# A mixer's chain, attention and merges given steps one whole unit apart, with the order left to the scheduler

## The chip, the cores and the metric

The kernel runs on one core of one Trainium2 chip. The metric is the device time of one execution in microseconds (us), less is better. Three executions of the kernel before took 1160.99, 1154.00 and 1153.95 us, median 1154.0.

## The reference

One layer of a streaming encoder on a stream of 16 meta tokens and 512 frames, width 1024, fp32: a half-step SwiGLU feed-forward (FFN1, inner width 2816), a mixing of two head groups side by side, a second half-step SwiGLU (FFN2) and a final norm.

```python
h += 1/2 * SwiGLU(RMSNorm(h))
n = RMSNorm(h); z = n @ W_in
h += concat(rwkv_out, attn_out) @ W_out
h += 1/2 * SwiGLU(RMSNorm(h))
```

`rwkv_out` is the RWKV-7 recurrence, 8 heads of 64, one state of 64x64 per head:

```python
sa = jnp.einsum('bhvk,bhk->bhv', S, -kk_t)
S = (S * w_t[:, :, None, :]
     + sa[..., None] * (kk_t * a_t)[:, :, None, :]
     + v_t[..., None] * k_t[:, :, None, :])
y_t = jnp.einsum('bhvk,bhk->bhv', S, r_t)
```

followed by a norm per head, a bonus term and a gate. `attn_out` is attention with 8 query and 2 key heads, in chunks of 64 frames with a window of two chunks back, the meta tokens, ALiBi and one sink per head.

## The kernel before, in words

The stream is cut in two halves of tokens: half 0 (A: the meta tokens and frames 0 to 255, 272 columns) and half 1 (B: 256 columns). Everything is held transposed, features on the partitions. Each weight matrix lies in tiles ("units"), most of 128 output features by 1024 inputs. A unit's weights come by DMA (`raw`), are rounded by ACT to a high part (`whi`, L122), and DVE takes the rest as a low part (`wlo`, L125); both are read on the fast fp32r path. A unit is 24 matmuls of 256 or 272 columns for a half ("main matmuls"): 16 with `whi` against the high and the low part of the activations (L213, L214), 8 with `wlo` against the high part (L195, for the down projection L222). Three buffers each for `raw`, `whi`, `wlo` are made by `prep` three units ahead.

`drive` walks the list of units: FFN1 of A; then, between units of FFN1 of B, the units of `w_in` of A, the mixing of A and `w_out` of A; then `w_in` of B, the units of FFN2 of A beside the mixing of B, `w_out` of B, the rest. After each unit it calls `advance(cost)`, which lets the side generators go on. A generator has a credit: each unit adds its cost, a step takes what the step yields, and steps run while the credit is positive. There are two generators in a mixing:

- `rwkv` is first the inverse of 40 + 40 unit-triangular blocks of 32x32 (`tinv`, a DVE loop of 31 steps, L726 and L728), then a round trip of the result through DRAM, whose DMAs the ACT queue issues (L734 to L746), then two steps of 32x32 matmuls, L753 and L761, that merge the blocks to 64x64 (called the merge here). `chain` then walks five chunks (the 16 meta tokens or one more of 64, then 64 tokens each): `values` (64x64 matmuls L791 and L796 and four copies L799, L800 per chunk); L813 and L816, copied by L819 and added by L820; L828, copied by L830; then L838 to L848, the state update L851 and L852 and the output Y (L855, L856). A group norm follows each chunk: square L869, matmul L872, root L874, reciprocal L875, products L877 to L879, and its result is written by L881 (ACT, high part) and L882 (DVE, low part) into `n0a` or `n1a`, an input of `w_out`.
- `attention` walks four chunks of a half, each in two steps (`mp2`): scores L910, masks and maxima on DVE (L916 to L920), exponential on ACT (L924), reciprocal L928, scaling by ACT (L929), transposes L930 and L932, copies L937 and L939, products L942 and L945, then L950 and L951 into `n0b` or `n1b`, the other inputs of `w_out`.

`w_out` reads `WO = (4, 5, 6, 7, 0, 1, 2, 3)`: blocks 4 to 7 (attention) first, then 0 to 3 (chain).

PSUM has a pool of main accumulators (`big`), one-bank tiles `mx` (two buffers) and one two-bank tile `as` (one buffer, `banks()`), which attention uses for scores, transposes and products. `values` takes two `mx`.

The order of each engine's queue is not the program's: the tile scheduler places instructions by their dependences and by priorities, which `PRIO` raises by 100 for chain and norm.

Of the kernel before, what the change touches and what calls it, by code (L numbers as in the profile page):

```python
# [9 lines left out]
AF = mybir.ActivationFunctionType  # L10
# [24 lines left out]
WARM = 12  # L35
TIW, CHW, ATW = 1.4, 0.55, 0.9
NK = D // 128
# [31 lines left out]
class Prog:  # L69
# [96 lines left out]
    def advance(self, cost):  # L166
        for sd in list(self.sides):
            if sd not in self.sides:
                continue
            sd[1] += cost  # L170
            while sd[1] > 0:
                self.mark(self.ph or sd[2] if sd[2] == 'rwkv' else sd[2])
                with self.tc.high_priority(PRIO.get(self.ph if sd[2] == "rwkv" else "", PRIO[sd[2]])):
                    c = next(sd[0], None)
                if c is None:
                    self.sides.remove(sd)
                    break
                sd[1] -= c
# [525 lines left out]
    def tinv(self, hf, mp, tip):  # L704

        nc, A, V, P, PE, t, GT = self.nc, self.A, self.V, self.P, self.PE, self.t, self.GT
# [17 lines left out]
        for k in range(1, 32):  # L724
            m = tmp[:n2, :k * k].rearrange("g (j s) -> g j s", s=k)
# [21 lines left out]
        self.ph = 'tizo'  # L747
        yield 6.0
        pc = [(p, c, slice((p * 4 + c - 1) * 32, (p * 4 + c) * 32)) for p in range(4) for c in range(1, 5)]
# [5 lines left out]
        for h in range(2):  # L755
            (A.copy, V.tensor_copy)[h](out=Z[hr[h]], in_=bz[hr[h]])
        yield 2.0
        bo = self.mbank()
# [3 lines left out]
        for h in range(2):  # L762
            (A.copy, V.tensor_copy)[h](out=GT[hr[h], 4 * h:4 * h + 4, 1:5, 32:64],
                                       in_=bo[hr[h]].rearrange("p (h s t) -> p h s t", h=4, s=4))
        yield 2.0

    def chain(self, hf, st, mo, cp):

        A, V, P, PE, t, GT, S = self.A, self.V, self.P, self.PE, self.t, self.GT, self.S
# [3 lines left out]
        def step():  # L773

            for n_ in list(norms):
                if next(n_, None) is None:
                    norms.remove(n_)
# [4 lines left out]
        def values(n):  # L782


            slot, tok, C = chunks[n]
            UV, BT = t(cp, [128, 2, 4, 64], "UV", bufs=2), t(cp, [128, 2, 4, 64], "BT", bufs=2)
            vr = (slice(64, 64 + C), slice(0, C))
            bs = [self.mbank() for h in range(2)]
            for p in range(4):
# [13 lines left out]
        values(0)  # L803
        yield CHW
        hp = [(p, h) for p in range(4) for h in range(2)]
        for n, (slot, tok, C) in enumerate(chunks):
# [5 lines left out]
            for p, h in hp:  # L812
                PE.matmul(X[ur[h], cols(p)], gt(vr, h, p, 0), UV[vr[h], h, p], start=True, stop=True)  # L813
            if slot:
                for p, h in hp:
                    PE.matmul(Z[hs[h], cols(p)], self.AR[p][hs[h], slot, 0:64], S[hs[h], p], start=True, stop=True)  # L816
# [7 lines left out]
            step()  # L824
            yield 2 * CHW
            X = self.mbank()
            for p, h in hp:
                PE.matmul(X[ur[h], cols(p)], gt(ur, h, p, 0), Rs[ur[h], cols(p)], start=True, stop=True)  # L828
            for h in range(2):
                (A.copy, V.tensor_copy)[h](out=UV[ur[h], h], in_=X[ur[h], 0:256].rearrange("p (j c) -> p j c", j=4))  # L830
            step()
            yield CHW
            if n + 1 < len(chunks):
                values(n + 1)
            yield CHW
            X, Z = self.mbank(), self.mbank()
# [16 lines left out]
            if slot:  # L853
# [3 lines left out]
                norms.append(self.group_norm(st, mo, cp, Y, slice(64 * slot - 64, 64 * slot)))  # L857
            step()
            yield 2 * CHW
        self.ph = 'gn'  # L860
        while norms:
            step()
            yield 2.0

# [20 lines left out]
    def attention(self, hf, st, mo, ap_):  # L885
        A, V, P, PE, t = self.A, self.V, self.P, self.PE, self.t
        for ci in range(4):
            c = 4 * hf + ci
            nw = min(c + 1, 3)
            W = 17 + 64 * nw  # L890
# [13 lines left out]
            A.copy(out=VK[0:81, 0], in_=b[0:81, 0:128])  # L904
            yield ATW
            kss = (slice(0, 64), slice(64, 128))
            for mp2 in range(2):
                bs, rows = self.banks(), []
# [3 lines left out]
                for kv in range(2):  # L912
                    g, x = 2 * kv + mp2, bs[kv][:, 0:W]
                    s = t(ap_, [128, 209], "s", bufs=2)
                    m = t(ap_, [128, 4], "m", bufs=4)
# [5 lines left out]
                    rows.append((s, m))  # L921
                yield ATW
                for s, m in rows:
                    A.activation(s[:, 0:W], s[:, 0:W], AF.Exp, bias=m[:, 2:3], accum_out=m[:, 3:4])  # L924
                yield ATW
                b, bo = self.banks()
                for kv, (s, m) in enumerate(rows):
                    V.reciprocal(m[:, 3:4], m[:, 3:4])  # L928
                    A.activation(s[:, 0:W], s[:, 0:W], AF.Copy, scale=m[:, 3:4])  # L929
                    PE.transpose(b[0:81, 256 * kv:256 * kv + 128], s[:, 0:81], self.ident)  # L930
                    if nw > 1:
                        PE.transpose(b[0:W - 81, 256 * kv + 128:256 * kv + 256], s[:, 81:W], self.ident)  # L932
                yield ATW
                pTs = []
# [8 lines left out]
                if nw > 1:  # L943
                    for kv, ks in enumerate(kss):
                        PE.matmul(bo[ks, 0:128], VK[0:W - 81, 1, ks], pTs[kv][0:W - 81, 1], start=False, stop=True)  # L945
                yield ATW
                ms, ts = slice(2 * mp2, 2 * mp2 + 2), slice(64 * ci, 64 * ci + 64)
# [3 lines left out]
                V.tensor_tensor(out=ml, in0=ov, in1=mh.bitcast(F32), op=ALU.subtract)  # L951
                yield ATW

# [250 lines left out]
```

## Time and profile before

| | |
|---|---|
| Executions | 1160.99, 1154.00, 1153.95 us; median 1154.0 |
| Profiled execution | 1158.89 us, of which span on the core 1156.7 us |
| Mean granted clock of TensorE | 0.971 |
| Busy: PE, DVE, ACT, POOL | 1114.7, 826.4, 673.0, 36.4 us |
| ACT table loads for L395, L924, L874 | 25, 13, 5, at 1283 ns |

The span is the time from the first to the last instruction of the profiled execution; 2.2 us lie around it. PE is TensorE's matmul stream, which is pipelined: a busy window may hold matmuls 0.12 us apart or, at half of the granted clock, some 0.21 us apart. So for PE three things are read: idle time and its releaser, the granted clock of a window (PEclk, 1.00 is 2.4 GHz and 0.50 is 1.2 GHz), and the number of matmuls in it.

### The profile page before, as it was taken

How to read it: one execution, taken by the hardware profiler on the slowest of the kernel's cores; microseconds unless marked ns; L12 is line 12 of the kernel's file. 1: busy time of each engine (PE TensorE's matmuls, PEld its weight loads, DVE VectorE, ACT ScalarE, POOL GpSimd, SP SyncE). 2: the span in 40 equal slices, each digit the busy share in tenths (PEclk: the TensorE clock that was granted, in tenths of full speed). 3: DMA queues.
4: the chain of work that ended last, by engine and by line, in shares of the span. 5: the costliest groups of instructions: out<-in, count | busy, mean ns of one | idle time of the engine just before them, and what ended most of it. 6: DMA issues, size and time to landing. Idle time of an engine off the chain costs nothing.

```text
span 1156.7 us, 23838 instructions
## 1 busy us (share of the span) xinstructions
PE 1114.7 (96%) x9621; PEld 1043.9 (90%) x9621; DVE 826.4 (71%) x1533; ACT 673.0 (58%) x1162; POOL 36.4 (3%) x91
## 2 busy tenths in 40 slices
PE   8999999999999998999899999997999899999996
PEld 7999999998999997899899898997889898888885
DVE  7866566776778993356888777995356677777666
ACT  7544444686757645565567685574456366545453
POOL 0000000021000000000002000000000000000000
PEclk8999999999999998899899999998899899999999
DMA  7565655544446554223355445556224356676661
GB/s 270 172 182 185 187 177 179 166 142 151 129 137 182 163 176 131 81 93 112 92 182 167 138 134 169 165 152 163 90 76 122 111 154 216 201 205 194 186 186 66
DMA packets 68721, 178.81 MB, mean 155 GB/s; under 512 B 21620, under 2 KB 26868, under 8 KB 68612
## 3 DMA queue, kind: packets, MB, share of 16 engines
q1 hardware_dynamic: 52384, 173.70, 49.1%
q10 hardware_dynamic: 16228, 3.61, 1.5%
q8 instruction: 75, 1.23, 0.4%
q14 instruction: 34, 0.28, 0.1%
HBM read 173.54 MB, written 3.74 MB: 153 GB/s over the span
## 4 chain that ended last, share of the span: by engine, by line
PE 76%; DVE 13%; DMA 4%; ACT 4%; issue 3%; ACTq 1%; SPq 0%; DVEq 0%
PE big L214 16%; PE big L213 16%; PE big L195 12%; PE big L201 10%; PE big L203 5%; DVE wlo L125 4%; PE big L222 4%; DVE tmp L726 3%; DVE rn L728 2%; PE mx L796 1%; ACT whi L122 1%; PE mx L791 1%; DMA d<-GT 1%; DMA res<-xT_in 1%; DMA d<-rn 1%
## 5 line engine op out<-in xcount | busy, mean ns | idle before, releaser
L122 ACT CAST whi<-raw 128x1024 fp32r<-128x1024 f32 (+1 forms) x321 | 334.8, 1045 | 279.0 <-PE big L214 146.8
L125 DVE TENSOR_TENSOR wlo<-raw,whi 128x1024 fp32r<-128x1024 f32 x320 | 389.7, 1219 | 119.0 <-ACT whi L122 96.2
L214 PE MATMUL big<-h,whi 128*128 128x256 f32 (+1 forms) x528 | 135.2, 289 | 0.0
L213 PE MATMUL big<-h,whi 128*128 128x256 f32 (+1 forms) x528 | 132.0, 288 | 0.0
L213 PE MATMUL big<-n0a,whi 128*128 128x272 f32 (+1 forms) x464 | 123.8, 296 | 8.2 <-ACT n0a L881 3.2
L214 PE MATMUL big<-n0a,whi 128*128 128x272 f32 (+1 forms) x464 | 123.1, 293 | 0.6 <-DVE n0a L342 0.6
L213 PE MATMUL big<-n0b,whi 128*128 128x272 f32 (+1 forms) x464 | 120.3, 290 | 0.4 <-ACT n0b L341 0.3
L214 PE MATMUL big<-n0b,whi 128*128 128x272 f32 (+1 forms) x464 | 119.7, 288 | 0.4 <-DVE n0b L342 0.4
L214 PEld LDWEIGHTS big<-h,whi 128*128 128x128 f32 x528 | 100.6, 191 | 1.5 <-issue 0.9
L213 PEld LDWEIGHTS big<-h,whi 128*128 128x128 f32 x528 | 99.7, 191 | 0.6 <-issue 0.3
L213 PEld LDWEIGHTS big<-n0a,whi 128*128 128x128 f32 x464 | 89.6, 194 | 10.6 <-ACT n0a L881 3.4
L214 PEld LDWEIGHTS big<-n0a,whi 128*128 128x128 f32 x464 | 90.0, 194 | 2.1 <-DVE n0a L342 1.0
L213 PEld LDWEIGHTS big<-n0b,whi 128*128 128x128 f32 x464 | 87.9, 190 | 2.0 <-ACT n0b L341 1.1
L214 PEld LDWEIGHTS big<-n0b,whi 128*128 128x128 f32 x464 | 87.8, 190 | 1.6 <-DVE n0b L342 0.7
L213 PE MATMUL big<-n1a,whi 128*128 128x256 f32 x288 | 76.9, 297 | 8.3 <-ACT n1a L881 4.2
L222 PE MATMUL big<-h,wlo 128*128 128x256 f32 (+1 forms) x528 | 81.3, 289 | 0.0
L195 PE MATMUL big<-n0b,wlo 128*128 128x272 f32 (+1 forms) x464 | 77.4, 288 | 0.0
L195 PE MATMUL big<-n0a,wlo 128*128 128x272 f32 (+1 forms) x464 | 76.4, 286 | 0.0
L214 PE MATMUL big<-n1a,whi 128*128 128x256 f32 x288 | 76.2, 293 | 0.0
L214 PE MATMUL big<-n1b,whi 128*128 128x256 f32 x288 | 76.1, 294 | 0.0
L213 PE MATMUL big<-n1b,whi 128*128 128x256 f32 x288 | 75.7, 292 | 0.0
L222 PEld LDWEIGHTS big<-h,wlo 128*128 128x128 f32 x528 | 71.5, 192 | 1.1 <-issue 0.6
(313 smaller groups left out, 2264.2 us busy)
## 6 DMA issues: line engine op xcount, KB each, us to landing
raw<-w_in SPq DMA_DIRECT2D x319, 512.0 KB, 3.8
outT<-o SPq DMA_DIRECT2D x8, 256.0 KB, 2.6
res<-xT_in SPq DMA_DIRECT2D x2, 544.0 KB, 4.3
res<-xT_in SPq DMA_DIRECT2D x2, 512.0 KB, 9.1
d<-GT ACTq DMA_DIRECT2D x8, 80.0 KB, 3.6
zk<-d ACTq DMA_DIRECT2D x2, 320.0 KB, 4.0
d<-rn ACTq DMA_DIRECT2D x2, 320.0 KB, 3.7
GT<-d ACTq DMA_DIRECT2D x8, 80.0 KB, 4.5
```

Of the source, the lines that this page charges most:

```text
L122: self.A.copy(out=hi[:, a:a + n], in_=raw[:, a:a + n])
L125: self.V.tensor_tensor(out=lo[:, 0:nk], in0=raw[:, 0:nk], in1=hi[:, 0:nk].bitcast(F32), op=ALU.subtract)
L195: self.PE.matmul(o, lo[:, k], x(k)[:, 0], start=False, stop=(k == ks[-1]))
L201: self.PE.matmul(o, hi[:, i], x(k).rearrange("p a t -> p (a t)"), start=(k == first), stop=False)
L203: self.PE.matmul(o[:, 0:256], lo[:, i], x(k)[:, 0], start=False, stop=(k == last))
L213: self.PE.matmul(o, w, x[:, 0], start=first, stop=False)
L214: self.PE.matmul(o, w, x[:, 1], start=False, stop=False)
L222: self.PE.matmul(o, lo[:, i], x(k)[:, 0], start=False, stop=(k == nk - 1))
L726: V.tensor_tensor(out=m, in0=NT[:n2, 0:k, k].unsqueeze(1).broadcast_to([n2, k, k]), in1=TI[:n2, 0:k, 0:k], op=ALU.mult)
L728: V.tensor_reduce(out=TI[:n2, 0:k, k], in_=m, op=ALU.add, axis=mybir.AxisListType.X)
L791: PE.matmul(b[vr[h], cols(p)], st["vT", p][hs[h], tok:tok + C], self.cent[hs[h], hs[h]], start=True, stop=True)
L796: PE.matmul(b[hs[r], cols(p, 256)], self.BK[p][hs[h], slot, hs[r ^ h]], self.ident[hs[h], hs[h]], start=True, stop=True)
```

## The change

A yielded `UNIT_END` ends a generator's turn: its credit is set to 0, and its next step comes after the next unit. Most steps of the merge, the chain and attention now yield it instead of a cost; the round trip's 6.0 is four of them. `values` takes its two banks from the tile `as`. L813 and L816 are issued in one loop, the norms' `step()` stands at the beginning of a chain step instead of its end, and in attention the reciprocal and the scaling stand right behind the exponentials, with two unit ends before the transposes.

```diff
-TIW, CHW, ATW = 1.4, 0.55, 0.9
+TIW = 1.4
+UNIT_END = -1.0
...
                 if c is None:
                     self.sides.remove(sd)
+                    break
+                if c == UNIT_END:
+                    sd[1] = 0.0
                     break
                 sd[1] -= c
...
         self.ph = 'tizo'
-        yield 6.0
+        for _ in range(4):
+            yield UNIT_END
...
-        yield 2.0
+        yield UNIT_END
         bo = self.mbank()
...
-            bs = [self.mbank() for h in range(2)]
+            bs = self.banks()
...
         values(0)
-        yield CHW
+        yield UNIT_END
...
                 PE.matmul(X[ur[h], cols(p)], gt(vr, h, p, 0), UV[vr[h], h, p], start=True, stop=True)
-            if slot:
-                for p, h in hp:
+                if slot:
                     PE.matmul(Z[hs[h], cols(p)], self.AR[p][hs[h], slot, 0:64], S[hs[h], p], start=True, stop=True)
...
             step()
-            yield 2 * CHW
+            yield UNIT_END
+            step()
             X = self.mbank()
...
-            step()
-            yield CHW
             if n + 1 < len(chunks):
                 values(n + 1)
-            yield CHW
+            yield UNIT_END
+            step()
             X, Z = self.mbank(), self.mbank()
...
-            step()
-            yield 2 * CHW
+            yield UNIT_END
         self.ph = 'gn'
         while norms:
             step()
-            yield 2.0
+            yield UNIT_END
...
-                yield ATW
                 for s, m in rows:
                     A.activation(s[:, 0:W], s[:, 0:W], AF.Exp, bias=m[:, 2:3], accum_out=m[:, 3:4])
-                yield ATW
+                for s, m in rows:
+                    V.reciprocal(m[:, 3:4], m[:, 3:4])
+                    A.activation(s[:, 0:W], s[:, 0:W], AF.Copy, scale=m[:, 3:4])
+                yield UNIT_END
+                yield UNIT_END
                 b, bo = self.banks()
                 for kv, (s, m) in enumerate(rows):
-                    V.reciprocal(m[:, 3:4], m[:, 3:4])
-                    A.activation(s[:, 0:W], s[:, 0:W], AF.Copy, scale=m[:, 3:4])
                     PE.transpose(b[0:81, 256 * kv:256 * kv + 128], s[:, 0:81], self.ident)
...
-                yield ATW
+                yield UNIT_END
```

The order on PE at the second merge (mixing B), before. `mx` and `as` are PSUM tiles, `t2c` and `Z` the blocks of the inverse, `vT` the values, `BK` the keys:

```order
L213 MATMUL big_10651<-h_1589_10639,whi_10541 128x256
L761 MATMUL mx_9218<-t2c_8995,Z_9153 32x32
L791 MATMUL mx_9259<-cent,vT_1152_7704 64x64
L761 MATMUL mx_9218<-t2c_8995,Z_9153 32x32 x2
L791 MATMUL mx_9259<-cent,vT_1176_7834 64x64
```

The same place on PE, after (L767 is L761 of before; the values, L797 and L802, stand some 250 main matmuls ahead):

```order
L218 MATMUL big_10569<-n0b_7311,whi_10448 128x256
L219 MATMUL big_10569<-n0b_7311,whi_10448 128x256
L767 MATMUL mx_9088<-t2c_8832,Z_9043 32x32
L200 MATMUL big_10569<-n0a_7310,wlo_10449 128x256 x4
L200 MATMUL big_10569<-n0b_7311,wlo_10449 128x256
L767 MATMUL mx_9088<-t2c_8832,Z_9043 32x32 x31
L200 MATMUL big_10569<-n0b_7311,wlo_10449 128x256 x3
L218 MATMUL big_10625<-h_1463_9859,whi_10484 128x256
```

Before, the pairs go on between the 64x64 matmuls to the end of both; after, the 32x32 matmuls are one run between main matmuls.

The order on PE where mixing B ends and `w_out` of B begins, before. `n1b` holds attention's results, `n1a` the chain's, L872 is the last chunk's norm:

```order
L213 MATMUL big_11250<-n1b_8107,whi_11137 128x256
L214 MATMUL big_11250<-n1b_8107,whi_11137 128x256
L872 MATMUL mx_9962<-gsq_9928,bones 128x256
L213 MATMUL big_11181<-n1a_8106,whi_11069 128x256
L213 MATMUL big_11215<-n1a_8106,whi_11106 128x256
L213 MATMUL big_11250<-n1a_8106,whi_11137 128x256
L214 MATMUL big_11181<-n1a_8106,whi_11069 128x256
```

The same place on PE, after. L935 and L937 are attention's transposes, L947 and L950 its last products:

```order
L937 MATMUL as_10683<-ident,s_10603 128x128
L935 MATMUL as_10683<-ident,s_10608 81x128
L937 MATMUL as_10683<-ident,s_10608 128x128
L947 MATMUL as_10683<-pT_10720,VK_10354 64x128
L947 MATMUL as_10683<-pT_10723,VK_10354 64x128
L950 MATMUL as_10683<-pT_10720,VK_10354 64x128
L950 MATMUL as_10683<-pT_10723,VK_10354 64x128
L218 MATMUL big_11172<-n1b_8102,whi_11060 128x256
L218 MATMUL big_11206<-n1b_8102,whi_11097 128x256
L218 MATMUL big_11241<-n1b_8102,whi_11128 128x256
```

The chain's last norm no longer stands there; it ended some 150 main matmuls earlier, and attention's last step stands directly in front of `w_out`.

The order on ACT in mixing B between two chunks' copies of `Rs`, before:

```order
L819 COPY Rs_9668<-mx_9650 128x256
L122 CAST whi_10970<-raw_10969 128x1024
L874 ACT_TABLE_LOAD
L874 ACTIVATE grs_9673<-mx_9671,dv 128x256
L395 ACT_TABLE_LOAD
L395 ACTIVATE silu_11032<-big_10975 128x256
L830 COPY UV_9536<-mx_9676 64x256
L799 COPY UV_9724<-mx_9726 64x256
L800 COPY BT_9725<-mx_9727 128x256
```

The stretch behind the copy of `Rs` on ACT, after (L927 is the exponential, L930 its scaling, L878 the norm's root):

```order
L824 COPY Rs_9726<-mx_9708 128x256
L124 CAST whi_10765<-raw_10764 128x1024
L927 ACT_TABLE_LOAD
L927 ACTIVATE s_9734,m_9735<-s_9734,m_9735 128x209
L927 ACTIVATE s_9739,m_9740<-s_9739,m_9740 128x209
L878 ACT_TABLE_LOAD
L878 ACTIVATE grs_9783<-mx_9781,dv 128x256
L836 COPY UV_9546<-mx_9786 64x256
L930 ACTIVATE s_9734<-s_9734,m_9735 128x209
L930 ACTIVATE s_9739<-s_9739,m_9740 128x209
```

Chain and attention lie closer together there, and the exponentials with their own table load stand in front of the chain's copy L836 (L830 before).

## Rows read from the trace of the kernel before

**Rows 1.** The page's first part: busy us, share of the span, instructions.

```profile
PE 1114.7 (96%) x9621; PEld 1043.9 (90%) x9621; DVE 826.4 (71%) x1533; ACT 673.0 (58%) x1162; POOL 36.4 (3%) x91
```

**Rows 2.** Windows: us, busy us of each engine (instructions), PEclk, DMA share, GB/s.

```profile
441.00:452.00 11.00, 10.76 (x97) 8.60 (x98) 5.33 (x7) 6.86 (x14) 0.00 (x0) 0.53 0.47 151
465.00:490.00 25.00, 25.00 (x222) 21.33 (x221) 8.51 (x24) 12.56 (x29) 0.00 (x0) 0.80 0.27 78
560.20:577.00 16.80, 12.99 (x78) 12.09 (x77) 14.47 (x28) 8.81 (x18) 0.10 (x1) 0.80 0.21 59
720.00:780.00 60.00, 59.29 (x502) 57.02 (x500) 59.53 (x114) 38.06 (x70) 3.60 (x6) 1.00 0.52 158
799.50:811.00 11.50, 7.07 (x64) 6.21 (x64) 4.72 (x9) 7.37 (x18) 0.00 (x0) 0.55 0.45 122
811.00:826.00 15.00, 15.00 (x146) 12.51 (x145) 4.16 (x17) 6.50 (x13) 0.48 (x2) 0.77 0.03 13
900.00:916.00 16.00, 11.84 (x76) 11.43 (x76) 9.20 (x19) 5.96 (x10) 0.00 (x0) 0.79 0.21 66
823.00:903.00 80.00, 79.93 (x1101) 72.98 (x1099) 48.21 (x99) 43.96 (x95) 0.00 (x0) 0.99 0.35 107
```

**Rows 3.** PE's waits over the span: us in total, times, longest.

```profile
PE as L930 <- ACT s L929: 8.8, 4, 5.0
PE big L213 <- ACT n1a L881: 4.2, 1, 4.2
PE big L213 <- ACT whi L122: 3.3, 2, 2.1
PE big L213 <- ACT n0a L881: 3.2, 1, 3.2
...
PE mx L753 <- DMA zk<-d: 1.4, 2, 1.2
```

**Rows 4.** Windows round bursts of small matmuls, columns as in rows 2.

```profile
454.50:455.60 1.10, 1.10 (x59) 1.04 (x58) 0.59 (x7) 0.64 (x3) 0.00 (x0) 1.00 0.82 78
468.70:472.20 3.50, 3.50 (x46) 2.34 (x45) 1.14 (x2) 0.86 (x4) 0.00 (x0) 1.00 0.43 105
476.30:481.20 4.90, 4.90 (x44) 3.72 (x44) 2.73 (x6) 3.49 (x10) 0.00 (x0) 0.80 0.34 107
509.30:510.60 1.30, 1.30 (x36) 1.11 (x35) 0.86 (x1) 1.29 (x3) 0.00 (x0) 1.00 0.00 0
813.20:820.90 7.70, 7.70 (x93) 5.64 (x92) 1.41 (x12) 2.87 (x7) 0.48 (x2) 0.76 0.01 2
```

**Rows 5.** ACT's timeline in the second merge: start, us, instruction, idle before.

```profile
785.62 0.32 ACTq L734 DMA_DIRECT2D d<-rn  x1
...
796.93 1.05 ACT L122 CAST whi<-raw 128x1024 fp32r<-128x1024 f32 x1 [6.65 <-DMA GT<-d]
```

**Rows 6.** ACT's groups in 790 to 905 us: busy us, mean ns, idle before.

```profile
L122 ACT CAST whi<-raw 128x1024 fp32r<-128x1024 f32 x19 | 19.9, 1046 | 16.3 <-DMA GT<-d 6.7 <-PE big L214 6.4 <-issue 1.8
...
L924 ACT ACTIVATE s<-s,m 128x209 f32<-128x209 f32 x8 | 3.7, 462 | 0.0
...
L800 ACT COPY BT<-mx 128x256 f32<-128x256 f32 x8 | 3.0, 372 | 0.0
...
L939 ACT COPY pT<-as 128x128 f32<-128x128 f32 x8 | 2.2, 276 | 0.0
```

**Rows 7.** ACT's timeline at a table load in the chain of B.

```profile
853.89 1.28 ACT L874 ACT_TABLE_LOAD   x1
855.19 0.47 ACT L874 ACTIVATE grs<-mx,dv 128x256 f32<-128x256 f32 x1
```

**Rows 8.** DVE's timeline over one attention step of B.

```profile
837.41 0.18 DVE L916 CUSTOM_DVE_ANT_0 s<-as,tabm 128x17 f32<-128x17 f32 x1 [0.72 <-PE as L910]
...
840.68 0.16 DVE L928 RECIPROCAL m<-m 128x1 f32<-128x1 f32 x1 [0.29 <-ACT s L924]
```

More of the change, by code (lines that the diff above doesn't have):

```diff
@@ L862, in chain @@
             step()
-            yield 2.0
+            yield UNIT_END
     def group_norm(self, st, mo, cp, Y, ts):
@@ L921, in attention @@
                     rows.append((s, m))
-                yield ATW
                 for s, m in rows:
                     A.activation(s[:, 0:W], s[:, 0:W], AF.Exp, bias=m[:, 2:3], accum_out=m[:, 3:4])
-                yield ATW
+                for s, m in rows:
+                    V.reciprocal(m[:, 3:4], m[:, 3:4])
+                    A.activation(s[:, 0:W], s[:, 0:W], AF.Copy, scale=m[:, 3:4])
+                yield UNIT_END
+                yield UNIT_END
                 b, bo = self.banks()
                 for kv, (s, m) in enumerate(rows):
-                    V.reciprocal(m[:, 3:4], m[:, 3:4])
-                    A.activation(s[:, 0:W], s[:, 0:W], AF.Copy, scale=m[:, 3:4])
                     PE.transpose(b[0:81, 256 * kv:256 * kv + 128], s[:, 0:81], self.ident)
@@ L932, in attention @@
                         PE.transpose(b[0:W - 81, 256 * kv + 128:256 * kv + 256], s[:, 81:W], self.ident)
-                yield ATW
+                yield UNIT_END
                 pTs = []
@@ L945, in attention @@
                         PE.matmul(bo[ks, 0:128], VK[0:W - 81, 1, ks], pTs[kv][0:W - 81, 1], start=False, stop=True)
-                yield ATW
+                yield UNIT_END
                 ms, ts = slice(2 * mp2, 2 * mp2 + 2), slice(64 * ci, 64 * ci + 64)
@@ L951, in attention @@
                 V.tensor_tensor(out=ml, in0=ov, in1=mh.bitcast(F32), op=ALU.subtract)
-                yield ATW
+                yield UNIT_END
 def program(tc, io, out):
```

## The prediction, made before the changed kernel ran

> **What bounds the kernel now.** I read the page's first part, then windows with the granted clock, PE's waits, and last the timelines of ACT and DVE where the windows show a loss. L numbers are those of the kernel before; a line of the changed file is marked so. The page says that PE is busy for 1114.7 of 1156.7 us [rows 1]: TensorE bounds, and another engine counts only where PE waits for it, where the granted clock falls, or where the order makes PE's own work longer. The window 720 to 780 us shows the good state: 59.29 of 60 us busy, clock 1.00, 502 matmuls at some 0.12 us each [rows 2]. The losses lie in few places of the two mixings, A (half 0, some 396 to 575 us) and B (half 1, some 770 to 916 us). The reader should see three kinds.
>
> First, waits. PE stands before L930 for ACT's scaling L929 (8.8 us in four waits, longest 5.0), before w_out for the last merge L881 (4.2 in B, 3.2 in A), before a main matmul for a cast L122 (longest 2.1), and for a DMA 1.4 [rows 3]. Second, half clock (1.2 of 2.4 GHz). In 441 to 452 us the mean granted clock is 0.53, in 799.5 to 811 it is 0.55; 465 to 490, 811 to 826, 560.2 to 577 and 900 to 916 show 0.80, 0.77, 0.80 and 0.79 [rows 2]. A window's length times one minus its clock is the time lost: 5.2, 5.2, 5.0, 3.5, 3.4, 3.4 us. Each of these windows holds a wait, or a burst of small matmuls whose tile size alternates. In 823 to 903 us, where most of B's chain runs beside attention, the clock is 0.99 and PE does not stand [rows 2]. Third, the alternation itself: 46 matmuls take 3.5 us at full clock where 64x64 and 16x16 tiles alternate, and 93 take 7.7 us where 32x32 and 64x64 do; 59 of a like size in one run take 1.10, and 36 take 1.30 where two 64x64 lines interleave [rows 4].
>
> **The change, term by term.** PE's order is the same up to main matmul 2847 (some 397 us), nearly the same between the mixings and the same after main 5880. No matmul is added or removed; ACT gets four table loads more.
>
> *Alternations go.* Before, L828 and L838 alternate with L791 and L796, and L761 with both. In the order after each of the three stands in one run (L767, L834 and L843 of the changed file; the 32x32 run with one matmul ahead of it, L843 twice broken by L802). Contiguous, 62 of the 32x32 kind cost 62 x 1.10/59 = 1.2 us and one of the 64x64 kind 1.30/36 = 0.036 [rows 4]. First place of A: 3.5 less 40 x 0.036 less six others at some 0.14 = 3.5 - 2.3 = 1.2 gained. Second: 4.9, of which 1.0 is the clock's (0.80), less 40 x 0.036 + 0.5 = 2.0 gained. B: 7.7, of which 1.85 is the clock's (0.76), less 1.2 + 24 x 0.036 + 1.0 (the L910s and three mains) = 2.75 gained. Sum **6.0**. With the bursts I let the half clock behind them go: 5.0 + 3.45 = **8.45**; the ends of this are 0 (it comes in any case) and 8.45. I take 8.45, as the later chunks, where there is no such burst, stand at full clock in 823 to 903.
>
> *End of mixing A.* Before, w_out(0) waits for L881 of the last chunk, the end of that chunk's norm, with the norm of the next stream between on DVE. After, the chain ends 200 main matmuls earlier (24 us), and what is late next is attention's last copy, a few main matmuls after its last products: two copies at 0.28 [rows 6] and what they queue behind, 0.8. Gain 3.2 + 3.4 clock - 0.8 = **5.8**; the other end is the whole 6.6.
>
> *Merges (the 32x32 steps).* ACT issues the DMAs of the inverse itself, and its casts stand behind them: in B from 785.62 to the cast at 796.93 [rows 5], 11.3 us with one cast between; A has the same issues. After, the issues stay on ACT in the same number and order, and SP's queue keeps its order. In the order a cast is some 56 main matmuls ahead of its use, 6.7 us, so a block of 10 to 11 us leaves PE short by 3 (A) and 4 (B); with it goes clock of some 4.2 each, between the 3.4 and 5.2 of [rows 2]: 15.4 in all. Before, these places cost 2.1 + 5.2 in A and 5.0 + 1.4 + 5.2 in B: 18.9. The four units in front of the first 32x32 step (11.5 us) hide the last DMA. Gain **3.5**; ends 18.9 and, as the block could find fewer casts in store than before, some -4.
>
> *What is added.* (1) The values of the first chunk are pulled in front of the inverse and hold the two-bank tile until they are copied out, which needs the chain's pool, opened only after the merge. Attention, whose scores, transposes and outputs need the same tile, stands still for 348 main matmuls in A and 248 in B. Nothing waits for it at once; it returns at the end. (2) The first L813 waits for the merge's copies and the values' copies, each queued on ACT behind a cast: 1.05 + 0.37 [rows 6], twice: **3.0**, the cover of the other small steps not counted; ends 0 and 3.0. (3) The chain is packed: from L813 of the first chunk to the last L876 there are 254 main matmuls in A instead of some 400. A chunk step's handoff is a copy of 0.37, with a unit (24 main matmuls x 0.12 = 2.9 us) and other steps to hide it. Where an attention step stands between, ACT does a table load 1.28, two exponentials 0.46 and a cast 1.05 in front of it [rows 6, 7], 3.3 us, and the transposes have 1 to 2 us of cover: I count two such places in A (2.1 and 2.5) and 0.9 of small ones in both: **5.5**; ends 0 and 8 x 2.7. One half-clock stretch after them, as at 560.2: **3.4** [rows 2]. (4) End of B: attention's last step now stands right in front of w_out(1). From its scores to the scaled probabilities 3.4 us on DVE and ACT (from 837.41 to 840.84) [rows 8], scaling 2 x 0.46, four copies at 0.28 and two more behind the products [rows 6], 1.7, and 1.0 for the transposes and products, estimated from the 0.036 of a small matmul and the 0.12 of a main one: 7.0, less 12 main matmuls of cover, 1.4 = 5.6. Before it was 4.2 [rows 3], with half clock behind either. Net **1.4**; ends -4.2 (the copies come in time) and 5.6. The reciprocal and scaling L929 right behind the exponentials cost nothing: the same instructions, and PE's queue before them is not held.
>
> Gains 6.0 + 8.45 + 5.8 + 3.5 = 23.75; losses 3.0 + 5.5 + 3.4 + 1.4 = 13.3. Net 10.45 less than the profiled execution's 1158.9: 1148.4. That execution lies 4.9 above the median of 1154.0, so the forecast is 1143.5. A difference of 1% (11.5 us) is about what a measurement of this kernel tells from no change.
>
> A rule speaks against the change. In the trace a table load is 1.28 us and the activation behind it starts 1.30 us after the load's start (from 853.89 to 855.19) [rows 7]. The Trainium skill (ScalarE: Activation LUTs, "What ACT_TABLE_LOAD costs") gives about 1283 ns for the load and 1380 ns more for a drain, 2.66 us in all, for every switch. By that page the load in the places of (3) would cost 1.4 us more at each of the two, and the forecast would be some 3 us higher; the row shows no such drain, so the sum stays.
>
> **Rivals.**
> *The clock's part is given back (1152).* The half clock of the first chunks comes not from the alternation but from the waits and small steps near it, and stays. For: in 441 to 452 us the clock is low with one cast's wait and no alternation [rows 2, 3]. Against: 823 to 903 us has hundreds of small matmuls and full clock [rows 2]. Then the 8.45 go: 1143.5 + 8.45 = 1152.
>
> *The merges are cured (1131).* With four units before the first product and one between the others, no exponential and no transpose stands in the merge's place, as L930 did for 5.0 us [rows 3]. Then the clock stays full there (8.4 of my 15.4), or the stall goes too: 1143.5 less 8.4 to 15.4 = 1135 to 1128, middle 1131. For: B's largest loss sits there, behind attention, which now stands still. Against: ACT's block of DMA issues is unchanged.
>
> *ACT becomes the bound of the packed chain (1182).* ACT works in order. Per 64-token chunk it has nine steps of the chain at 0.37 to 0.46 (3.8), a table load for the root 1.28, two casts 2.1, and with an attention step a second load 1.28, two exponentials and two scalings 1.84, five copies at 0.28 (1.4): 11.7 us [rows 6, 7], beside some 47 main matmuls (5.6 us) and 9 us of small matmuls on PE. It fits on average, but a step whose copy stands behind load, exponentials and cast is late by 3.3 less a cover of 0.6 = 2.7. If that happens in each of the eight chunks and half clock (3.4) follows each, it costs 8 x 6.1 = 49 instead of the 8.9 counted: 1143.5 + 40 = 1183, say 1182. It decides from 2.4 us per chunk (8.9 and the net 10.5, over 8) against before, from 3.9 per chunk against the 1% bound. For: table loads rise from 7 to 12 in A's chain and from 5 to 8 in B's. Against: before, chain and attention ran in 823 to 903 us with hardly a loss.
>
> **How the numbers follow.** Forecast (own range 1138 to 1150) 0.45, of which 0.20 lies under 1142.5; merges cured 0.22; clock given back 0.13; ACT the bound 0.20. So faster by over 1%: 0.20 + 0.22 = 0.42; within 1%: 0.25 + 0.13 = 0.38; slower by over 1%: 0.20. The range reaches from the far end of the cured merges, 1128, to 1165, where the slow case in weaker form begins; some 0.2 stays outside, nearly all above.
>
> **What would show it.** Right: L767, L834 and L843 in single runs of 0.7 to 1.2 us; no low clock in the first chunk's stretch; no wait for the norm's L885 in front of w_out(0); in front of w_out(1) a wait of about 5 to 6 us for attention's copy L955 instead (lines of the changed file). In the merges, waits of 3 and 4 us for casts. Wrong: repeated waits of PE for the chain's copies (L824, L836, L805) or the scaling L930 of the changed file, a granted clock under 0.9 over its whole length, ACT busy over nine tenths there; or merges without a wait.

## The result and the profile after

The changed kernel took 1140.72 us (median of four, 1139.14 to 1143.30) against 1153.97: ratio 0.9875, 95% interval 0.9831 to 0.9919. It is faster by 1.25%; the forecast was 1143.5 within 1128 to 1165. The profiled execution took 1143.30 us, span 1140.5, against 1158.89 and 1156.7. PE was busy for 1084.7 us instead of 1114.7 [rows 1], though its instructions are the same 9621. PE's idle time rose, from 42.0 to 55.8 us: what went is time in which PE counts as busy.

Windows of the changed kernel, columns as in [rows 2]: the first merge, the first chunks of A, the end of A, the second merge, the end of B.

```profile
430.00:447.00 17.00, 10.65 (x125) 10.01 (x125) 5.44 (x6) 6.19 (x8) 0.00 (x0) 0.80 0.57 157
465.00:490.00 25.00, 22.18 (x424) 19.96 (x425) 12.00 (x30) 16.88 (x37) 0.00 (x0) 1.00 0.23 81
553.00:570.00 17.00, 16.47 (x138) 15.84 (x137) 14.03 (x25) 10.29 (x16) 0.10 (x1) 1.00 0.56 173
775.00:800.00 25.00, 19.33 (x227) 18.21 (x226) 9.70 (x14) 8.53 (x15) 0.00 (x0) 0.73 0.65 181
...
880.00:898.00 18.00, 14.78 (x86) 12.78 (x87) 5.20 (x20) 7.27 (x18) 0.00 (x0) 0.72 0.17 48
```

In 465 to 490 us the clock is 1.00 (0.80 before), with 424 matmuls instead of 222 in the same time (91 of them main ones, 86 before), and the end of A stands at 1.00 (0.80 before). The merges are still low, 0.80 and 0.73, and so is the end of B, 0.72 in 18 us (0.79 in 16 before).

PE's waits over the span (total, times, longest), against [rows 3]:

```profile
PE big L218 <- ACT whi L124: 13.4, 3, 6.3
PE as L935 <- ACT s L930: 8.0, 3, 3.6
PE mx L843 <- ACT grs L878: 4.7, 3, 2.5
PE mx L844 <- DVE UV L836: 3.3, 5, 1.4
PE big L315 <- DVE acc L310: 2.7, 2, 2.5
PE as L947 <- ACT pT L944: 2.6, 2, 1.8
```

The norm's waits in front of `w_out` (4.2 and 3.2) are gone. New are waits for casts, 6.3 in the first merge and 5.7 in the second, waits in the chain (L843, L844), and waits at attention's end in B. Here are ACT's timeline in the first merge and, behind it, PE's:

```profile
424.22 1.05 ACT L124 CAST whi<-raw 128x1024 fp32r<-128x1024 f32 x1 [1.10 <-DVE rn L733]
424.25 0.32 ACTq L739 DMA_DIRECT2D d<-rn  x1
...
435.29 0.52 ACTq L751 DMA_DIRECT2D t2c<-d  x1
436.19 1.99 ACT L124 CAST whi<-raw 128x1024 fp32r<-128x1024 f32 x2 [10.92 <-DMA t2c<-d]
```

```profile
430.31 0.64 PE L200 MATMUL big<-n1b,wlo 128*128 128x256 f32 x4
437.29 0.58 PE L218 MATMUL big<-n1a,whi 128*128 128x256 f32 x1 [6.34 <-ACT whi L124]
```

The cast that ended at 425.27 fed PE up to 430.95. ACT then issued DMAs until 435.81, and the next cast began at 436.19: no cast for 11 us, PE idle for 6.34.

A finer account: the time from the start of one main matmul to that of another, counted in PE's timeline of the profiled execution (us). The main matmuls' order is the same in all kernels; small matmuls that move to another stretch take their time with them, so a row's sum tells more than one column.

| kernel | A: inverse, merge 2832–3192 | A: chain –3648 | A: end –3744 | between –5040 | B: inverse, merge –5304 | B: first chunk –5400 | B: chain –5664 | B: end –5736 |
|---|---|---|---|---|---|---|---|---|
| before | 61.6 | 101.8 | 19.7 | 184.2 | 47.9 | 29.4 | 57.7 | 16.1 |
| after | 57.1 | 100.4 | 13.6 | 188.1 | 46.3 | 27.0 | 51.4 | 18.3 |
| unit ends, one-bank values | 58.1 | 104.2 | 14.3 | 186.1 | 41.8 | 22.9 | 57.3 | 14.9 |
| merge alone | 57.6 | 97.7 | 18.8 | 184.1 | 47.2 | 23.3 | 56.5 | 14.0 |
| attention alone | 57.3 | 99.0 | 19.4 | 184.2 | 42.7 | 29.0 | 57.5 | 15.1 |
| merge and attention | 57.1 | 97.8 | 18.4 | 184.4 | 42.0 | 22.9 | 58.1 | 16.1 |
| after, six more unit ends | 57.9 | 91.4 | 11.9 | 187.2 | 44.6 | 20.7 | 54.9 | 9.6 |
| after, twelve more unit ends | 56.8 | 98.7 | 11.9 | 186.0 | 40.6 | 16.8 | 62.0 | 10.0 |

Before main matmul 2832 and behind 5736 all of them agree within 0.5 us (the last stretch to 7128: 225.6 to 225.7 us). Of the profiled difference of 16 us, 12.0 come from A and 8.1 from B, and 3.9 are given back between, in a stretch where PE's order did not change: PE waits 2.5 us for L310 of the next norm (the row of L315 above), and 3.6 instead of 1.9 in front of an earlier attention step's transposes. The profiled execution of before lies 4.9 us above its median and that of after 2.6, so a column is good to a few us.

The same stretches of PE's trace can be split by kind: idle time before matmuls; time lost to half clock while PE was busy (busy time times one minus the granted clock); and the rest, which is PE's work counted at full clock. Here are the two mixings together (main matmuls 2832 to 3744 and 5040 to 5736), in us of the profiled execution, with the number of neighbours in PE's order that use parts of TensorE's array of different size, as the timeline prints them (128*128, 64*64, 32*32 and so on). The matmuls are the same in all rows.

| kernel | time | idle | half clock | work at full clock | changes of size |
|---|---|---|---|---|---|
| before | 334.1 | 18.3 | 22.9 | 292.9 | 263 |
| before, two-bank values | 327.9 | 32.6 | 20.3 | 274.9 | 195 |
| unit ends, one-bank values | 313.5 | 15.6 | 15.2 | 282.7 | 207 |
| after | 314.1 | 30.1 | 14.7 | 269.3 | 167 |
| merge alone | 315.0 | 17.0 | 8.0 | 290.0 | 235 |
| attention alone | 320.0 | 16.2 | 14.5 | 289.3 | 243 |
| after, six more unit ends | 291.1 | 14.0 | 5.9 | 271.2 | 175 |

Work falls with the changes of size, by some 0.25 us for each (23.6 us for 96 from before to after). The first four rows are the change's two parts in all four combinations. The two-bank values take 13 to 18 us of work and add 14 us of idle time, with unit ends or without; the unit ends take 6 to 10 us of work and add no idle time. The half clock has to be read with care: over whole executions the granted clock of the kernel before was between 0.970 and 0.981 (some 35 to 22 us lost), and the profiled one, with 0.971, lies near the lower end.

### The profile page after: what moved, and what is told of

It reads as the page before. It is cut to its first block, busy times and chain, and to the rows that moved or that the text cites. A ratio compares the mean times of both kernels' runs of the same rounds, so it can differ in the third digit from the quotient of the medians.

```text
span 1140.5 us, 23845 instructions
## 1 busy us (share of the span) xinstructions
PE 1084.7 (95%) x9621; PEld 1022.1 (90%) x9621; DVE 826.8 (72%) x1533; ACT 674.6 (59%) x1166; POOL 31.6 (3%) x91
## 4 chain that ended last, share of the span: by engine, by line
PE 79%; DVE 8%; ACT 6%; DMA 3%; issue 3%; ACTq 1%; DVEq 0%; SPq 0%
PE big L218 19%; PE big L219 18%; PE big L200 13%; PE big L206 11%; PE big L208 5%; PE big L227 5%; DVE wlo L127 2%; ACT whi L124 2%; DVE tmp L731 2%; DVE rn L733 1%; DMA zk<-d 1%; ACT s L927 1%; PE as L914 1%; DMA d<-rn 1%; ACT L927 1%
## 5 line engine op out<-in xcount | busy, mean ns | idle before, releaser
L219 PE MATMUL big<-h,whi 128*128 128x256 f32 (+1 forms) x528 | 133.0, 285 | 0.0
L218 PE MATMUL big<-h,whi 128*128 128x256 f32 (+1 forms) x528 | 130.8, 286 | 1.4 <-ACT whi L124 1.4
L218 PE MATMUL big<-n0b,whi 128*128 128x272 f32 (+1 forms) x464 | 121.7, 293 | 0.8 <-ACT n0b L955 0.4
L219 PE MATMUL big<-n0b,whi 128*128 128x272 f32 (+1 forms) x464 | 121.3, 291 | 0.4 <-DVE n0b L347 0.4
L218 PEld LDWEIGHTS big<-h,whi 128*128 128x128 f32 x528 | 98.5, 189 | 2.8 <-ACT whi L124 1.6
L219 PEld LDWEIGHTS big<-h,whi 128*128 128x128 f32 x528 | 99.3, 189 | 1.3 <-issue 0.9
L218 PEld LDWEIGHTS big<-n0b,whi 128*128 128x128 f32 x464 | 89.4, 194 | 2.3 <-ACT n0b L346 0.9
L219 PEld LDWEIGHTS big<-n0b,whi 128*128 128x128 f32 x464 | 89.3, 193 | 1.4 <-DVE n0b L347 0.7
L227 PE MATMUL big<-h,wlo 128*128 128x256 f32 (+1 forms) x528 | 78.6, 284 | 0.4 <-DVE wlo L127 0.4
```

Source lines behind the costliest of these rows:

```text
L218: self.PE.matmul(o, w, x[:, 0], start=first, stop=False)
L219: self.PE.matmul(o, w, x[:, 1], start=False, stop=False)
L227: self.PE.matmul(o, lo[:, i], x(k)[:, 0], start=False, stop=(k == nk - 1))
```

## The experiments

**All unit ends, but a chunk's values in two `mx` banks again.**

```diff
-            bs = self.banks()
+            bs = [self.mbank() for h in range(2)]
```

> The change without its PSUM part: steps lie a unit apart, but a chunk's values take two one-bank tiles again. In its order the alternations of 32x32, 16x16 and 64x64 matmuls are gone, attention goes on during the inverse as before, and the chain of B ends in front of w_out(1) as before. Theory (the alternations and the half clock behind them are the larger part of the gain): 12 to 14 us less than before, 1140 to 1144, with B's wait of 4 us for the last norm still there. Rival (the gain comes from the values in the two-bank tile, which lets the chain end early): no change, 1152 to 1156.

Measured: 1140.59 us, ratio to before 0.9896 (0.9869 to 0.9924): the whole gain of the change. In the first table B's merge and first chunk are 12.6 us shorter than before, and the wait for the last norm (4.2) is there as foreseen. One unit of A took 17.3 us: PE waited 3.20 for the bank of a norm, and 5.1 us of half clock followed. PE's row, then ACT's:

```profile
507.17 0.79 PE L797 MATMUL mx<-cent,vT 64*64 64x64 f32 x5 [3.20 <-ACT grs L878]
```

```profile
505.35 1.28 ACT L878 ACT_TABLE_LOAD   x1
506.64 0.47 ACT L878 ACTIVATE grs<-mx,dv 128x256 f32<-128x256 f32 x1
```

PE starts 0.06 us after the root L878 has read its bank: of the two `mx` banks that the values need, one is held by the norm until a table load and the root are done.

**Only the values in the two-bank tile, in the kernel before.**

```diff
-            bs = [self.mbank() for h in range(2)]
+            bs = self.banks()
```

> Only the PSUM part of the change in the kernel before: a chunk's values in the two-bank tile, the old costs. In its order the chain stands behind attention and its last four chunks are squeezed into 200 main matmuls in front of w_out(0), and into 60 in B. Theory (the parts need each other; without the unit ends the shared tile makes the chain wait for attention): slower than before by the latency of a chunk's chain, some 10 to 15 us for 3 to 5 chunks in each half less the main matmuls between, 40 to 90 us more, 1190 to 1240. Rival (the two-bank tile is what gains): 1140 to 1146.

Measured: 1150.89 us, ratio 0.9974 (0.9958 to 0.9991). Neither expectation held. The chain was squeezed in front of `w_out` as the order says, and the ends of both mixings grew, A's to 33.8 us and B's to 42.0, but the stretches that it left shrank by nearly as much (A's chain 89.6, B's first chunk 13.7, B's chain 42.3). In the second table 14.3 us more waiting stand against 18.0 us less work. The latency of a chunk that I had put at 10 to 15 us was too high; PE's largest new wait there is for the norm's square:

```profile
PE mx L872 <- ACT gsq L869: 7.5, 2, 5.1
```

**The inverse's DMAs on GpSimd's queue.**

```diff
-nc.scalar.dma_start(
+nc.gpsimd.dma_start(
```

(in all seven places of `tinv`)

> The changed kernel with the inverse's DMAs issued by GpSimd's queue and not ScalarE's. Theory (PE stood 6.3 and 5.7 us in the merges because casts stood behind these issues on ScalarE): both waits for L124 go, and the half clock behind them, 1.6 + 1.8 and 1.8 + 4.0 + 1.1 us less one half for what stays: 12 + 5 us less, 1120 to 1128. Rival (the casts wait for weights or buffers): waits of the same length, 1139 to 1143. GpSimd's issue may be slower, then the merges come later but PE doesn't wait there.

Measured: 1174.75 us, ratio 1.0197 (1.0164 to 1.0230). The waits for casts left the list of waits, and ACT's timeline has five casts between 433.5 and 444.9 us, while GpSimd issues the DMAs: so those waits did come from the issues on ACT. But a wait for the DMAs took their place. PE's wait, then GpSimd's timeline:

```profile
PE mx L759 <- DMA zk<-d: 37.5, 4, 17.5
```

```profile
431.27 0.54 POOL L739 DMA_DIRECT2D d<-rn  x1 [76.01 <-DVE rn L733]
...
435.69 0.74 POOL L745 DMA_DIRECT2D GT<-d  x1 [1.40 <-DMA d<-rn]
441.49 0.70 POOL L745 DMA_DIRECT2D GT<-d  x1 [5.06 <-issue]
...
461.81 0.69 POOL L750 DMA_DIRECT2D zk<-d  x1 [1.96 <-issue]
```

GpSimd's issues of the 80 KB blocks start 2.7 to 5.8 us apart, and the round trip from L739 to the last issue takes 30.5 us (11.6 on ACT's queue, from 424.25 to 435.81). PE's order was fixed for a shorter one.

**Twelve more unit ends in front of the first values.**

```diff
+        for _ in range(12):
+            yield UNIT_END
         values(0)
         yield UNIT_END
```

> The changed kernel with twelve more unit ends in front of the first chunk's values, so that in the program attention's steps come before them. In its order attention goes on during the inverse, attention ends 190 and 80 main matmuls before w_out, the chain 110 and 50. Theory (the first values hold the two-bank tile, attention stands still and comes back in front of w_out(1)): the waits at the end of B (L935 1.6, L947 2.6, L955 0.7 us) and the half clock there, some 4 us, go, and little is lost elsewhere: 8 us less, 1130 to 1135. Rival (attention's place doesn't matter, its waits move into the chain): 1139 to 1145.

Measured: 1123.07 us, ratio 0.9741 (0.9704 to 0.9778), 17.6 us below the change where 8 were expected, so below the theory's range too. Its windows round the first merge's DMAs and at the end of B, then its waits:

```profile
427.00:438.00 11.00, 10.40 (x88) 10.20 (x86) 6.37 (x17) 1.05 (x1) 0.00 (x0) 1.00 0.79 220
...
850.00:880.00 30.00, 28.27 (x301) 26.26 (x300) 20.87 (x45) 21.17 (x38) 0.00 (x0) 1.00 0.38 111
```

```profile
PE mx L845 <- ACT grs L880: 4.6, 3, 2.5
PE as L937 <- ACT s L932: 4.6, 4, 1.9
...
PE big L218 <- ACT whi L124: 1.1, 1, 1.1
```

The end of B stands at full clock and takes 10.0 us instead of 18.3, as expected. What I had not foreseen: the waits for casts in the merges go too (1.1 left of 12.0), and ACT's timeline has a cast at 428.89 between its first DMA issue of the merge (428.45) and the next (432.10).

**Six instead of twelve** (`range(6)`).

> The changed kernel with six more unit ends in front of the first values instead of twelve. In its order attention goes on during the inverse as with twelve, but ends 105 main matmuls before w_out(0) (190 with twelve) and 21 before w_out(1) (80). Theory (attention standing still during the inverse, and its end right at w_out(1), cost the time): most of the gain, 1124 to 1131; what is left is a wait of up to 3 us for attention's copies in front of w_out(1). Rival (only the full delay, which shifts the whole chain, helps): 1135 to 1142.

Measured: 1120.30 us, ratio 0.9708 (0.9688 to 0.9727): the fastest kernel of this study. One wait for a cast (4.1 us) is back in a merge, the chain of A is shorter than with twelve (91.4 against 98.7), and the end of B has no wait of note. So the delay need not be as long as the inverse; it must only let attention's steps come first.

**The alternation by itself.** In the changed kernel 64 additional matmuls of 64x64 stand in each merge, between the pairs of 32x32 products, or behind them in one run (`bd` is one more bank; nothing reads it):

```diff
             for h in range(2):
                 PE.matmul(bo[hr[h], o], Z[hr[h], o], T2c[hr[h], p, c], start=True, stop=True)
+            for h in range(2):
+                PE.matmul(bd[dq[h], 0:64], self.ident[dq[h], dq[h]], self.cent[dq[h], dq[h]], start=True, stop=True)
```

> The changed kernel with 64 more 64x64 matmuls in each merge (rows of the profile; their result is read by nothing), set between the pairs of 32x32 products: 16 alternations. Theory (changing the tile size between neighbours costs PE time): the burst takes 16 periods of 0.45 to 0.5 us, 7 to 8 us, against some 3.5 us where the same matmuls stand in two runs. Rival (the bursts before were slow because of the clock or of waits alone): 3 to 4 us here too, at full clock.

> The same 64 additional 64x64 matmuls in each merge, in the program behind the run of 32x32 products: the counterpart of the alternating kernel. Theory and rival both: 1.2 us for the 32x32 run and 2.3 us for the 64x64 run at full clock.

Measured: 1160.62 and 1143.23 us, one execution each. PE's timeline of the alternating kernel, one period, then the runs of the other:

```profile
448.07 0.25 PE L768 MATMUL mx<-t2c,Z 32*32 32x32 f32 x4
448.25 0.33 PE L770 MATMUL mx<-cent,ident 64*64 64x64 f32 x4
448.51 0.25 PE L768 MATMUL mx<-t2c,Z 32*32 32x32 f32 x4
```

```profile
448.45 1.19 PE L768 MATMUL mx<-t2c,Z 32*32 32x32 f32 x62
449.57 2.08 PE L771 MATMUL mx<-cent,ident 64*64 64x64 f32 x64
```

A period is 0.44 us, and the whole burst 7.5 us, in which the clock falls near its end (0.71 in the last 2.1 us, 1.00 before); in two runs the same matmuls take 3.2 us. The theory's price holds for these bursts. In the two runs the eight matmuls of a period take 0.20 us, so each of a period's two changes of size costs 0.12 us. Most of the 17 us between the two kernels lies elsewhere; it was not taken apart.

**The unit ends in the merge alone**, chain and attention as before:

```diff
-        yield 6.0
+        for _ in range(4):
+            yield UNIT_END
...
-        yield 2.0
+        yield UNIT_END
...
         values(0)
-        yield CHW
+        yield UNIT_END
```

> The kernel before with the unit ends in the merge alone, and one behind the first values; chain and attention keep their costs. Its order loses the alternation of 32x32 with 64x64 in B (32 changes of tile size between small matmuls fall to 9) and keeps that of 16x16 with 64x64 in A (25 to 19). Theory (the alternations are the gain): B's 2.75 us of burst and 3.45 us of half clock go, 6 us less than before, 1146 to 1149. Rival (the even spacing of chain and attention is the gain): 1152 to 1155.

Measured: 1143.18 us, ratio 0.9906 (0.9875 to 0.9936), more than the theory's 6 us: neither range held. B's first chunk took 23.3 us instead of 29.4: 6.1, the sum expected (2.75 + 3.45). Yet in A the alternations of L834 and L844 with the values stayed, and the half clock did not. Its windows of A's first chunks and B's:

```profile
465.00:490.00 25.00, 25.00 (x284) 20.81 (x284) 11.24 (x37) 14.50 (x31) 0.00 (x0) 1.00 0.28 86
800.00:826.00 26.00, 26.00 (x381) 23.39 (x381) 12.23 (x39) 15.31 (x38) 0.48 (x2) 0.99 0.33 103
```

So in A the half clock of [rows 2] did not hang on those bursts alone. By the second table nearly all that this kernel gains against the profiled execution of before is half clock (8.0 instead of 22.9).

**The unit ends in attention alone**, with the scaling behind the exponentials; merge and chain keep their costs.

> The kernel before with the change in attention alone: unit ends, and the scaling right behind the exponentials. The merge and the chain keep their costs; its order keeps the alternations (29 of 32 changes of tile size between small matmuls in B, 20 of 25 in A). Theory (merges and alternations carry the gain, attention's spacing none): within 4 us of the kernel before, 1149 to 1157. Rival (any even spacing gains, as the merge alone and all of them gave nearly the same): 1141 to 1147.

Measured: 1142.69 us, ratio 0.9891 (0.9860 to 0.9922): the rival's number. In its order the alternations stay, and B's first chunk keeps its 29.0 us. What it gains in B is another thing: its merge takes 42.7 us instead of 47.9, since no transposes of attention stand between the 32x32 products any more. PE's longest wait before them is 1.9 us; in the kernel with unit ends in the merge alone it is still 5.2. The row of the one, then of the other:

```profile
PE as L936 <- ACT s L931: 2.6, 2, 1.9
```

```profile
PE as L936 <- ACT s L935: 9.8, 5, 5.2
```

**Both of these together**, without the chain's unit ends.

> The kernel before with the unit ends of the merge and those of attention, but the chain's old costs and its values in one-bank tiles. Theory (the two parts each remove one loss in B, the alternation and the wait of the transposes in the merge, and so add up there; what all unit ends without the two-bank tile lost again, 3.2 us of wait for the norm's bank and 5.1 us of half clock behind it in one unit of A, comes from the packed chain): 6 to 9 us below the kernel with unit ends everywhere and one-bank tiles (1140.6), 1131 to 1135. Rival (any of the parts gives the same 11 us and no more, whichever it is): 1139 to 1144.

Measured: 1136.93 us, ratio 0.9866 (0.9809 to 0.9923), between the two expectations, and its interval overlaps those of either part. The first table tells more: in B both gains stand side by side (42.0 and 22.9), and A's chain takes 97.8 us against 104.2 with the chain's unit ends and one-bank values. By time alone it stays open.

**Twelve more unit ends, values in `mx` banks.**

> The kernel with twelve more unit ends (1123.1), with a chunk's values in two one-bank tiles instead of the two-bank tile. Its chain is drawn out again: it ends 23 main matmuls before w_out(0) and behind the start of w_out(1)'s attention blocks. Theory (the two-bank tile gains once attention does not stand still for it, since the chain then ends early in both halves): 10 to 16 us more, 1133 to 1139, with the wait for the norm's L887 of some 3 to 4 us back in B. Rival (the tile is neutral, as 1140.6 with one-bank tiles against 1140.7 says): 1121 to 1126.

Measured: 1133.98 us, ratio 0.9831 (0.9800 to 0.9861): the theory's number. The two-bank tile is worth 11 us once attention does not stand still for it; with unit ends alone it is worth nothing, and in the kernel before 3 us (ratio 0.9974). Two of its waits, for the next norm and for the chain's last:

```profile
PE big L315 <- DVE acc L310: 4.0, 2, 2.5
PE big L218 <- ACT n1a L887: 3.5, 1, 3.5
```

**Twelve more unit ends, the norm's step at the end of a chain step.**

```diff
             yield UNIT_END
-            step()
...
+            step()
             yield UNIT_END
```

(for the three steps of a chunk)

> The kernel with twelve more unit ends in front of the first values, with the norm's step back at the end of a chain step, as before the change, so that on ScalarE the copy of a chunk's products comes in front of the root and its table load. Theory (PE stands 4.6 us in three waits before the third chain step because that copy stands behind the root's table load): these waits go, 4 to 6 us less than that kernel's 1123.1: 1117 to 1119. Rival (the wait moves to the next instruction behind the table load): 1121 to 1126.

Measured: 1124.79 us, ratio 0.9742 (0.9715 to 0.9768), the rival's number; the waits stayed (4.9 us in three). The scheduler still put the copy behind the root, so the edit did not test what it should. But the rows name the cause. ACT, then PE:

```profile
493.72 1.28 ACT L880 ACT_TABLE_LOAD   x1
495.01 0.47 ACT L880 ACTIVATE grs<-mx,dv 128x256 f32<-128x256 f32 x1
495.39 0.35 ACT L837 COPY UV<-mx 64x256 f32<-64x256 f32 x1
```

```profile
495.54 0.67 PE L844 MATMUL mx<-UV,BT 64*64 64x64 f32 x15 [2.47 <-ACT grs L880]
```

PE starts at 495.54, after the root's end (495.48) and before the copy's (495.74): it waited for the norm's `mx` bank, not for the copy, whose rows of `UV` L844 does not read.

## Why the prediction was right, point by point

*The sum.* The time came out within 3 us of the forecast, but not by the sizes of its terms. By kind, the terms say 6.0 us less work, 10.45 less half clock and 6.0 more waiting. In the profiled executions the two mixings have 23.6 less work, 8.2 less half clock and 11.8 more waiting, and 3.9 are given back between them. Two terms were too small, the alternations by a factor of four and the waits by two, and their errors have opposite signs: that the number is so near is in part luck. The half clock is weaker still: over whole executions the granted clock was 0.973 to 0.977 in the changed kernel's four and 0.977 in the median of thirteen of the kernel before, so less half clock in all is not shown.

*Alternations, 6.0 and 8.45 of clock.* The mechanism was right, the 6.0 too small: I priced three bursts, but changes of size went away along both mixings, 96 of 263. At the 0.12 us of the additional bursts this would be 12 us of the 23.6. Over the twelve kernels with the same matmuls the work of a mixing follows the number of changes within some 1.4 us, at 0.26 us each, an estimate from their traces; why a change takes more there than in those bursts is open. The half clock was right for B, shown by its first chunk with the merge's unit ends alone (6.1 us against 2.75 + 3.45), and the price is shown by itself. In A it was not shown to be the bursts': with the bursts in place the window stood at 1.00. That part of the term came out for a reason that I did not give, and which is not settled.

*End of mixing A, 5.8.* Right: 19.7 to 13.6 us, 6.1.

*Merges, 3.5 gained with stalls of 3 and 4 us.* The mechanism was right, the stalls were 6.3 and 5.7:

```profile
PE big L218 <- ACT whi L124: 5.7, 1, 5.7
```

The step that was mis-sized is the store of casts set against the block: the last cast lasted 5.7 us of PE's work, not 6.7, and the block on ACT ran 11 us with no cast inside, where before one stood in it. The half clock behind them (3.4 us in A; 6.8 in B, from 775 to 800 us, 25 times 0.27) was near 4.2 in A and above it in B. So stalls and clock cost 22.2 us, more than the 18.9 of before, and this term taken alone was a loss. That the two columns still fell, by 4.5 and 1.6, is work that left them.

*L813's waits, 3.0.* Did not come: PE's list has no wait at this line.

*The packed chain, 5.5 and 3.4 of clock.* Waits in 452 to 530 us are 2.8 + 2.7 + 1.0 = 6.5, in 800 to 853 2.0 + 2.3 = 4.3: twice the term. Not quite half of it is a wait that I had not named, PE for a PSUM bank that the norm holds until the table load and the root are done (L843 behind L878, 4.7 in all). The half clock was 3.4 in A's chain, as taken, and none in B's.

*End of B, net 1.4.* The waits are 1.64 + 0.85 + 1.75 and two of 0.36, 5.0 in all against 5.6 forecast:

```profile
879.94 0.44 PE L947 MATMUL as<-pT,VK 81*64 81x128 f32 x4 [1.75 <-ACT pT L944]
...
886.53 0.34 PE L935 MATMUL as<-ident,s 128*81 128x128 f32 x1 [1.64 <-ACT s L930]
...
888.18 0.69 PE L947 MATMUL as<-pT,VK 81*64 81x128 f32 x4 [0.85 <-ACT pT L944]
```

The stretch took 18.3 us instead of 16.1, 2.2 more. L955, which I had named for this wait, stands for only 0.7 of it.

*Given back between the mixings.* 3.9 us, not in the sum.

*The rivals.* ACT did not become the bound: in 465 to 490 us it is busy for 16.9 of 25. The clock's part was not given back in the chunks (1.00 in 465 to 490 and in 800 to 853 us), though over whole executions the clock is no higher than before. Of the signs of being wrong, waits for L836 and L930 did come, in a small form: 3.3 us in five and 8.0 in three, one of these between the mixings. The merges were not cured by the change; the two kernels with more unit ends show what their cure and attention's place are worth, 18 to 20 us. That the two-bank tile makes attention stand still was foreseen; that "nothing waits for it at once" was true, but the time it cost was not counted: the casts missing in the merges and the end of B. With six more unit ends the work stays low (271.2) and the idle time falls from 30.1 to 14.0.

*What the change is made of.* Its gain does not need its PSUM part (1140.6 without). Against the runs of before beside them, the merge alone gave 10.5 us, attention alone 11.6, both 16.0 and all unit ends 12.7. With one-bank values, the bank's wait and the half clock behind it cost 8.3 us in one unit of A, which the kernel without the chain's unit ends does not have; with the two-bank tile the work falls by 13.4 us more, and the idle time rises by 14.5: the casts in the merges, the chain's waits and B's end. Why A fell by several us in each of these kernels alike is open in part: with the merge alone, attention alone or both, A's work and idle time stay within some 2 us of before, and what falls is half clock (13.5 us to 3.1 to 6.0). In the profiled execution of before the clock was 0.971, in the median one 0.977, which makes some 7 us of 1157.

## What to carry to other kernels

Small matmuls of different tile sizes should stand in runs: alternating them cost more than twice the time of the same matmuls (7.5 against 3.2 us), and spacing the steps that issue them is enough to separate them. A shared single-buffer tile serves its users in program order, so a step that is written early and runs late blocks the others from its place in the program on; put it where it will run (17.6 to 20.4 us here). Look at what an order puts directly in front of a consumer, and at how many buffers of work a queue has in store when it is blocked by DMA issues. And check a forecast by kinds, waiting, half clock and work, and not by its total alone: here an error of some 18 us in the work was mostly hidden by errors of 6, 4 and 2 us the other way, in the waits, between the mixings and in the half clock.

## What the runs showed of the hardware

A change of the array's size between neighbouring matmuls cost 0.12 us in the additional bursts, and some 0.26 us by the comparison of the kernels' traces. The half clock of some 3.4 us or more came behind idle stretches of 2 to 6 us, but not always: in the changed kernel PE waited 2.5 us for a bank in 470 to 500 us and 2.05 in 800 to 853, and the clock of both windows is 1.00. Bursts of alternating tile sizes of some 4 us were seen both with half clock behind them and without; the one of 7.5 us ended in it. DMAs of the same size landed in similar time from both queues (`GT<-d`, median 6.2 us from ACT's issue in the changed kernel, 4.6 from GpSimd's), but GpSimd issued these 4.4 to 5.8 us apart, where ACT put four issues into 3.15 us.
